# Modulation products in four column strips of TensorE, the first norm in two halves, and row broadcasts by transposes

## Chip, cores and metric

One core of one Trainium2 chip. The metric is the device time of one execution in microseconds, the median of several runs.

## The reference, cut to what matters

Two transformer blocks run one after the other on 256 tokens of width 1024, each of two layers, all in float32. The first has two streams, x (256 tokens) and ctx (256 tokens), and modulates its norms with vectors that come from two condition vectors c and c_ctx:

```
silu_c = silu(c);  silu_cc = silu(c_ctx)
for l in range(2):
    mod   = silu_c  @ w_mod[l] + b_mod[l]          # 6 * 1024 values
    mod_c = silu_cc @ w_mod[l] + b_mod[l]
    sh1, sc1, g1, sh2, sc2, g2 = split(mod, 6)      # the same of mod_c
    h  = rms_norm(x,   norm1[l]) * (1 + sc1)  + sh1
    hc = rms_norm(ctx, norm1[l]) * (1 + csc1) + csh1
    ... = split(h @ w_in[l]), split(hc @ w_in[l])   # q, k, v of two attentions, gates
    x  = x + g1 * branch_merge(attention a, attention b, gates)
    x  = x + g2 * swiglu(rms_norm(x, norm2[l]) * (1 + sc2) + sh2)   # ctx alike in layer 0
return second_block(rms_norm(x, final_norm))
```

The second block has per layer a feed-forward part, a mixer of three attentions, and another feed-forward part, with RMS norms and no modulation.

## The kernel before

Activations lie transposed: 128 partitions by 8 k-tiles by tokens. A float32 product of full accuracy is made of three products of the faster type fp32r: every operand is split into a high part (`hi`, ScalarE, line 403) and a remainder (`lo`, VectorE, line 408), and `group` (with `matmuls`, line 427) issues high x high, high x low and low x high. Weights come from HBM in pieces of up to 1024 columns of float32 per partition (`Weights.raw`, line 341, issued on SyncE's queue, tag "raw", five buffers), and `Weights.next` splits them into eight buffers of high and eight of low parts.

The modulation vectors are products of two rows (the silu of c and of c_ctx, `self.sc`) with w_mod, 512 columns at a time, made in three ways. `mod_columns` makes ten column groups of layer 0. Eight of them go through the split: the stationary operand is `self.scr` (four columns: two high, two low), the moving one is the high and then the low part of the weights, 16 matmuls of 512 columns in all. Two (numbers 1 and 3 of the first four, `MOD_EXACT`, line 610) use plain float32, with `self.sc` (two columns) as the stationary operand. Either way the result is copied to SBUF (line 620), brought into columns by four transposes (line 623), added up by a reduction (line 625) and given its bias (`mod_bias`, line 644). The other columns (layer 0's last two groups and all of layer 1) are multiplied on VectorE (`mod_rest`), and the change doesn't touch them.

`mod_first` makes the first four groups (shift of k-tiles 0 to 3, scale of 0 to 3, shift of 4 to 7, scale of 4 to 7), loads stream x ahead of the first and ctx ahead of the second (`load_x`: load, sums of squares by transposes, reciprocal root by Newton steps, multiply), and works out the amplitude after each pair. `block1` then calls `norm_mod` for each stream, which goes through four blocks of two k-tiles and writes the high and low part of the norm. `b1_attention` then runs layer 0's tokens in the order of `B1_ORDER[0]`: it begins with the value product V1 (k-tiles in order, first stream x, then ctx), and among the later tokens M0 to M5 are the other six groups of `mod_columns` (weights "wm1").

`rows` turns two columns of 128 numbers into rows that are the same on all partitions: a float32 matmul with the column, broadcast along the free dimension, as the stationary operand and the identity as the moving one (line 542). It is called for every reciprocal root that is spread (`spread`), in `keys` and in `forget_rows` of the mixer. `b1_keys` has the same form four times (line 928).

Instructions are put in order by a scheduler that simulates the engines, on the basis of program order and readiness; each engine then runs its own list strictly in that order.

Of the kernel before, what the change touches and what calls it, by code (L numbers as in the profile page):

```python
# [30 lines left out]

BANKS = {"mm": 3, "s": 2, "y": 3}
NPT = (1, 2)
MOD_EXACT, MOD_X = (1, 3), (0, 1)
SUB = 512


# [155 lines left out]

def pieces(n, kparts):

    most = RAW // n // (SUB // n) * (SUB // n)
    return [min(most, nk - k) for nk in kparts for k in range(0, nk, most)]


# [167 lines left out]
class Builder:  # L367
# [171 lines left out]
    def rows(self, ps, r):  # L539

        for t in range(2):
            i = self.nc.tensor.matmul(  # L542
                ps[:, t * P : (t + 1) * P], r[:, t : t + 1].broadcast_to((P, P)), self.ident, start=True, stop=True
            )
        return i

    def spread(self, r, hold=None):
# [9 lines left out]
        self.hold(1, self.last_step, hold[2])  # L557
        return self.spread(self.r, hold[1])

    def norm_mod(self, l, which, i, x, h, pool, rsb=None):  # L560


        nc, (hh, hl) = self.nc, h
        A, B = self.amp[l][:, i, 8 * which :], self.mod[l][:, i, 24 * which :]
        c = slice(i * SEQ, (i + 1) * SEQ)
        for k in range(0, NKT, 2):
            t = pool.tile([P, 2, SEQ], F32, tag="nt", name=self.u("nt"), bufs=3)
            src = x[:, k : k + 2]
            if rsb is not None:
                nc.vector.tensor_tensor(t, src, rsb.unsqueeze(1).broadcast_to((P, 2, SEQ)), ALU.mult)  # L570
                src = t
            for j in range(2):
                a, b = A[:, k + j : k + j + 1], B[:, k + j : k + j + 1]
                if i or j:
                    nc.scalar.activation(t[:, j], src[:, j], AF.Identity, bias=b, scale=a)  # L575
                else:
                    nc.vector.tensor_scalar(t[:, j], src[:, j], a, b, ALU.mult, ALU.add)
            self.hi(hh[:, k : k + 2, c], t)
            self.last_norm = self.lo(hl[:, k : k + 2, c], t, hh[:, k : k + 2, c])
# [6 lines left out]
    def setup_mod(self):  # L586
        nc, cp = self.nc, self.cp
        self.sc = cp.tile([P, NKT, 2], F32, name="sc")
        a = PAR["c"][0]
        nc.scalar.activation(  # L590
            self.sc, self.par[:, a : a + 16].rearrange("p (w k) -> p k w", w=2), AF.Silu
        )
        self.scr = cp.tile([P, NKT, 4], F32R, name="scr")
        self.hi(self.scr[:, :, 0:2], self.sc)
        self.lo(self.scr[:, :, 2:4], self.sc, self.scr[:, :, 0:2])

        self.mod = [cp.tile([P, 2, 48], F32, name=f"mod{l}") for l in range(2)]

        self.amp = [cp.tile([P, 2, 16], F32, name=f"amp{l}") for l in range(2)]

    def mod_columns(self, w, c, tile, exact=None):

        nc = self.nc
        (ps,) = self.product()
        if exact:
            n = 2
            for kp in range(4):
                t = w.raw(2, 512, "mraw", exact)
                for k in range(2):
                    nc.tensor.matmul(  # L610
                        ps[:n], self.sc[:, 2 * kp + k], t[:, k * 512 : (k + 1) * 512],
                        start=(kp, k) == (0, 0), stop=(kp, k) == (3, 1), skip_group_check=True,
                    )
            w.i += 1
        else:
            n = 4
            wk = w.next()
            self.matmuls([(0, 0, ps[:n], self.scr[:, k], a) for k in range(NKT) for a in wk(k)])
        row = tile("mrow")[:n]
        nc.scalar.copy(row, ps[:n])  # L620
        tp = self.bank("y")
        for i in range(4):
            nc.tensor.transpose(tp[:, n * i : n * i + n], row[:, i * P : (i + 1) * P], self.ident[:n, :n])
        a, b = c // P, c // P + 4
        nc.vector.tensor_reduce(
            self.mod[0][:, :, a:b], tp[:, : 4 * n].rearrange("p (j h c) -> p c j h", h=n // 2, c=2), AX.X, ALU.add
        )
        self.mod_bias(0, a, b, 2)

    def mod_first(self, pool):  # L630

        w = Weights(self, "wm0")
        tile = lambda name: pool.tile([P, 512], F32, tag=name, name=self.u(name), bufs=2)
        for i, c in enumerate(MOD_FIRST):
            if i in MOD_X:
                self.load_x(MOD_X.index(i), pool)
            self.mod_columns(w, c, tile, pool if i in MOD_EXACT else None)
            if i % 2:
                self.amplitude(0, 0, 2, slice(2 * i - 2, 2 * i + 2))

    def mod_bias(self, l, c0, c1, nw):
        b = self.p(f"bmod{l}")[:, c0:c1]
# [153 lines left out]
    def block1(self, layers, fill):  # L796
        nc = self.nc
        with self.open("y0") as yp:
            y = self.y_tiles(yp, 2 * SEQ)
            w = Weights(self, "wb1_0")  # L800
            with self.open("h0") as hp:
                h = self.inputs_of(hp)
                with self.open("n0", "right") as np_:
                    self.xs = []
                    self.mod_first(np_)
                    for i, x in enumerate(self.xs):
                        self.norm_mod(0, 0, i, x, h, np_)
                with self.open("a0", "right") as self.ap_:
                    gates = self.b1_attention(0, w, *h, y, 2 * SEQ, yp)
            self.xs, self.xstack = [], ExitStack()  # L810
# [103 lines left out]
    def b1_keys(self, l, w, full, cos, sin):  # L914
# [10 lines left out]
        pr = self.bank("y")  # L925
        for t in range(4):
            o = slice(t * P, (t + 1) * P)
            nc.tensor.matmul(pr[:, o], rw[:, o], self.ident, start=True, stop=True)
        nc.vector.tensor_tensor(kc, kc, pr, ALU.mult)
        self.rope(kc[:, :SEQ], kc[:, :SEQ], cos, sin, SWAP1)  # L930
        return self.stack_k(kc, 512)
# [878 lines left out]
```

## Time and profile before

| | us |
|---|---|
| median of 3 runs | 2501.16 (2499.57 to 2503.38) |
| the profiled execution | 2499.92, span 2498.1 |
| TensorE busy | 2440.1 (98%) |
| VectorE busy | 1836.9 (74%) |
| ScalarE busy | 1373.1 (55%) |
| HBM read | 389.42 MB, 156 GB/s over the span |

In a row of a window the engines stand in the order PE, PEld, DVE, ACT, POOL (GpSimd). PE is TensorE, PEld its weight loads, DVE is VectorE, ACT ScalarE, SPq SyncE's queue of DMA issues. The span is that of the instructions of one execution; the execution's own time lies 1.8 us above it. The granted clock of TensorE (PEclk) is given as a share of full speed: 1.00 is 2.4 GHz, and a lower mean over a stretch says for how much of it the engine had the lower of its two levels, 1.2 GHz. A matmul's record lasts longer than its share of the array's time, since the next starts before it ends; the distance between two starts is what it costs amid other work.

### The profile page before, as it was taken

Reading aid. Unit: us, or ns where it says so; the run is one execution under the profiler, and the core shown is the slowest. Engines: PE = TensorE matmul, PEld = TensorE weight load, DVE = VectorE, ACT = ScalarE, POOL = GpSimd, SP = SyncE. Lnnn points to the kernel's source line nnn. Section 1 sums busy time; section 2 is a strip of 40 time slices with the busy share of each in tenths; the row PEclk is TensorE's granted clock in tenths of the full one; section 3 lists DMA queues with packets and bytes.
Section 4 is the critical chain, followed back from the end, with each engine's and each line's share of the span. In section 5 each row is a group of like instructions: output and inputs, shape, how many; then the busy total and the mean of one; then the engine's idle time right before and its main releaser. Section 6 shows DMA issues by size and latency. Waiting matters only on the chain.

```text
span 2498.1 us, 46101 instructions
## 1 busy us (share of the span) xinstructions
PE 2440.1 (98%) x17342; PEld 2257.4 (90%) x17342; DVE 1836.9 (74%) x4131; ACT 1373.1 (55%) x2683; POOL 0.2 (0%) x4
## 2 busy tenths in 40 slices
PE   8999999999999999999999999999999999999997
PEld 4877768888888898999999999999999999999997
DVE  6677886885766889876676687786666668778665
ACT  5566763422233667665555566755555556665553
POOL 0000000000000000000000000000000000000000
PEclk9999999999999999999999999999999999999999
DMA  7221453454654433565555553356666655336553
GB/s 265 92 72 56 147 178 137 159 184 141 208 183 135 127 115 106 155 187 182 182 185 182 184 182 109 113 178 186 181 186 186 183 180 184 100 116 190 184 180 102
DMA packets 112543, 393.46 MB, mean 157 GB/s; under 512 B 12480, under 2 KB 13760, under 8 KB 111808
## 3 DMA queue, kind: packets, MB, share of 16 engines
q1 hardware_dynamic: 112320, 390.52, 49.1%
q8 instruction: 136, 2.23, 0.4%
q14 instruction: 87, 0.71, 0.1%
HBM read 389.42 MB, written 1.05 MB: 156 GB/s over the span
## 4 chain that ended last, share of the span: by engine, by line
PE 95%; DVE 3%; ACT 2%; issue 0%; DMA 0%; SPq 0%; DVEq 0%; ACTq 0%
PE mm L427 84%; PE y L427 2%; PE s L427 2%; PE s L778 1%; PE y L785 1%; PE s L731 1%; PE y L542 1%; PE y L486 0%; PE mm L610 0%; PE y L678 0%; ACT nt L575 0%; DVE lwmx L408 0%; ACT k L403 0%; DVE kl L408 0%; DVE lwm L408 0%
## 5 line engine op out<-in xcount | busy, mean ns | idle before, releaser
L427 PE MATMUL mm<-hh,hwb 128*128 128x512 f32 (+2 forms) x1176 | 348.5, 341 | 2.6 <-ACT gt L1008 1.4
L427 PE MATMUL mm<-hl,hwb 128*128 128x512 f32 (+1 forms) x1176 | 347.5, 340 | 0.1
L427 PE MATMUL mm<-hh,lwb 128*128 128x512 f32 (+2 forms) x1176 | 347.0, 340 | 0.0
L403 ACT ACTIVATE hwb<-wb_0r 128x512 fp32r<-128x512 f32 (+1 forms) x250 | 149.6, 611 | 253.0 <-PE mm L427 243.5
L427 PE MATMUL mm<-gh,hwf 128*128 128x256 f32 x1344 | 269.5, 281 | 0.0
L427 PE MATMUL mm<-gh,lwf 128*128 128x256 f32 x1344 | 269.1, 281 | 0.0
L427 PE MATMUL mm<-gl,hwf 128*128 128x256 f32 x1344 | 268.4, 281 | 0.0
L408 DVE TENSOR_TENSOR lwf<-wf_1r,hwf 128x512 fp32r<-128x512 f32 (+1 forms) x272 | 183.4, 676 | 109.1 <-ACT hwf L403 100.1
L408 DVE TENSOR_TENSOR lwf<-wf_0r,hwf 128x512 fp32r<-128x512 f32 (+1 forms) x272 | 183.3, 675 | 102.9 <-ACT hwf L403 93.1
L403 ACT ACTIVATE hwf<-wf_1r 128x512 fp32r<-128x512 f32 (+1 forms) x272 | 168.2, 619 | 162.9 <-PE mm L427 149.3
L403 ACT ACTIVATE hwf<-wf_0r 128x512 fp32r<-128x512 f32 (+1 forms) x272 | 168.2, 619 | 162.2 <-PE mm L427 146.5
L427 PEld LDWEIGHTS mm<-hh,hwb 128*128 128x128 f32 x1176 | 204.0, 189 | 29.0 <-ACT gt L1008 2.4
L408 DVE TENSOR_TENSOR lwb<-wb_0r,hwb 128x512 fp32r<-128x512 f32 (+1 forms) x250 | 163.4, 665 | 86.2 <-ACT hwb L403 83.3
L427 PEld LDWEIGHTS mm<-hl,hwb 128*128 128x128 f32 x1176 | 203.7, 189 | 25.5 <-DVE hl L408 0.7
L427 PEld LDWEIGHTS mm<-hh,lwb 128*128 128x128 f32 x1176 | 204.1, 189 | 25.0
L403 ACT ACTIVATE hwb<-wb_1r 128x512 fp32r<-128x512 f32 (+1 forms) x242 | 146.2, 611 | 112.2 <-PE mm L427 101.6
L427 PEld LDWEIGHTS mm<-gh,hwf 128*128 128x128 f32 x1344 | 206.4, 188 | 0.0
L427 PEld LDWEIGHTS mm<-gh,lwf 128*128 128x128 f32 x1344 | 206.4, 188 | 0.0
L427 PEld LDWEIGHTS mm<-gl,hwf 128*128 128x128 f32 x1344 | 206.1, 188 | 0.0
L408 DVE TENSOR_TENSOR lwb<-wb_1r,hwb 128x512 fp32r<-128x512 f32 (+1 forms) x242 | 158.3, 666 | 63.2 <-ACT hwb L403 60.1
L427 PE MATMUL mm<-gl,hwmx 128*128 128x256 f32 x656 | 138.9, 289 | 3.3 <-DVE gl L408 3.3
L427 PE MATMUL mm<-actl,hwf 128*128 128x256 f32 x704 | 141.8, 283 | 0.0
(414 smaller groups left out, 5680.9 us busy)
## 6 DMA issues: line engine op xcount, KB each, us to landing
wf_0r<-in_wf_dram SPq DMA_DIRECT2D x120, 512.0 KB, 3.6
wf_1r<-in_wf_dram SPq DMA_DIRECT2D x120, 512.0 KB, 3.5
wb_0r<-in_wb_dram SPq DMA_DIRECT2D x108, 512.0 KB, 3.7
wb_1r<-in_wb_dram SPq DMA_DIRECT2D x105, 512.0 KB, 3.6
wmx_0r<-in_wmx_dram SPq DMA_DIRECT2D x49, 512.0 KB, 3.6
wmx_1r<-in_wmx_dram SPq DMA_DIRECT2D x49, 512.0 KB, 3.6
wm2r<-in_wm_dram SPq DMA_DIRECT2D x48, 512.0 KB, 3.5
wm1r<-in_wm_dram SPq DMA_DIRECT2D x24, 512.0 KB, 4.0
```

The source lines that it names most:

```text
L403: self.nc.scalar.activation(out, src, AF.Copy, scale=scale)
L408: return self.nc.vector.tensor_tensor(out, src, h, ALU.subtract)
L427: i = nc.tensor.matmul(out, lhsT, rhs, start=bank not in first, stop=n[bank] == 0, skip_group_check=True)
L542: i = self.nc.tensor.matmul(ps[:, t * P : (t + 1) * P], r[:, t : t + 1].broadcast_to((P, P)), self.ident, start=True, stop=True)
L731: nc.tensor.matmul(out, q[a], k[b], start=start and n == 0, stop=stop and n == 2, skip_group_check=True)
L778: nc.tensor.matmul(s[:, :nk], q[:, o], part, start=n == 0, stop=n == 1, skip_group_check=True)
L785: nc.tensor.transpose(tp[:, j * P : (j + 1) * P], pt[:, j * P : (j + 1) * P], self.ident)
```

## The change

All ten groups of `mod_columns` become plain float32 products. The stationary operand is `self.scp`, the two silu columns padded with zeros to 32, and k-tile k writes its products into partitions 32 (k mod 4) to 32 (k mod 4) + 31 of the PSUM bank, which is the strip of 32 columns of the array at the same place; k-tiles 4 to 7 add to those of 0 to 3. The copy takes all 128 partitions, and four float32 products with `self.four` (ones at the places of the four strips) add the strips and bring them into columns. Two additions with the bias read the result from PSUM. The weights go from the load buffers straight to TensorE: the first four groups have eight buffers of their own (tag "mraw"), the six of attention use the five of tag "raw". `mod_first` loads both streams ahead of the first group and calls `norm_mod` for k-tiles 0 to 3 of both streams after the second group, for 4 to 7 after the fourth. In `rows` and `b1_keys` the matmul with the identity becomes TensorE's transpose of the same operand.

```diff
-MOD_EXACT, MOD_X = (1, 3), (0, 1)
@@ def rows
-            i = self.nc.tensor.matmul(
-                ps[:, t * P : (t + 1) * P], r[:, t : t + 1].broadcast_to((P, P)), self.ident, start=True, stop=True
-            )
+            i = self.nc.tensor.transpose(ps[:, t * P : (t + 1) * P], r[:, t : t + 1].broadcast_to((P, P)), self.ident)
@@ def norm_mod
-        for k in range(0, NKT, 2):
+        for k in ks:
@@ def setup_mod
-        self.scr = cp.tile([P, NKT, 4], F32R, name="scr")
-        self.hi(self.scr[:, :, 0:2], self.sc)
-        self.lo(self.scr[:, :, 2:4], self.sc, self.scr[:, :, 0:2])
+        self.scp = cp.tile([P, NKT, 32], F32, name="scp")
+        nc.vector.memset(self.scp, 0.0)
+        nc.vector.tensor_copy(self.scp[:, :, :2], self.sc)
+        self.four = cp.tile([P, 2], F32, name="four")
+        nc.vector.tensor_tensor(self.four, self.ident[:, 0:2], self.ident[:, 32:34], ALU.add)
+        for j in (64, 96):
+            nc.vector.tensor_tensor(self.four, self.four, self.ident[:, j : j + 2], ALU.add)
@@ def mod_columns
-        if exact:
...
-        else:
-            n = 4
-            wk = w.next()
-            self.matmuls([(0, 0, ps[:n], self.scr[:, k], a) for k in range(NKT) for a in wk(k)])
-        row = tile("mrow")[:n]
-        nc.scalar.copy(row, ps[:n])
+        for k in range(NKT):
+            if k % 2 == 0:
+                t = w.raw(2, 512, *pool)
+            j, o = k % 4, 512 * (k % 2)
+            nc.tensor.matmul(
+                ps[32 * j : 32 * j + 32], self.scp[:, k], t[:, o : o + 512], start=k < 4, stop=k >= 4,
+                skip_group_check=True,
+            )
+        w.i += 1
+        row = tile("mrow")
+        nc.scalar.copy(row, ps)
         tp = self.bank("y")
-        for i in range(4):
-            nc.tensor.transpose(tp[:, n * i : n * i + n], row[:, i * P : (i + 1) * P], self.ident[:n, :n])
-        a, b = c // P, c // P + 4
-        nc.vector.tensor_reduce(
-            self.mod[0][:, :, a:b], tp[:, : 4 * n].rearrange("p (j h c) -> p c j h", h=n // 2, c=2), AX.X, ALU.add
-        )
-        self.mod_bias(0, a, b, 2)
+        self.matmuls([(0, i, tp[:, 2 * i : 2 * i + 2], row[:, i * P : (i + 1) * P], self.four) for i in range(4)])
+        a = c // P
+        for i in range(2):
+            nc.vector.tensor_tensor(
+                self.mod[0][:, i, a : a + 4], tp[:, i:8:2], self.p("bmod0")[:, a : a + 4], ALU.add
+            )
@@ def mod_first
-            if i in MOD_X:
-                self.load_x(MOD_X.index(i), pool)
-            self.mod_columns(w, c, tile, pool if i in MOD_EXACT else None)
+            if i == 0:
+                for x in range(2):
+                    self.load_x(x, pool)
+            self.mod_columns(w, c, tile, "mraw", pool, RAW, 8)
             if i % 2:
                 self.amplitude(0, 0, 2, slice(2 * i - 2, 2 * i + 2))
+                for x in range(2):
+                    self.norm_mod(0, 0, x, self.xs[x], h, pool, ks=(2 * i - 2, 2 * i))
@@ def block1
-                    self.mod_first(np_)
-                    for i, x in enumerate(self.xs):
-                        self.norm_mod(0, 0, i, x, h, np_)
+                    self.mod_first(np_, h)
@@ def b1_keys
-            nc.tensor.matmul(pr[:, o], rw[:, o], self.ident, start=True, stop=True)
+            nc.tensor.transpose(pr[:, o], rw[:, o], self.ident)
```

`pieces` also takes at least one k-tile per load now.

## Rows read from the trace of the kernel before

**Rows 1.** The page's busy shares: engine, busy us, share of the span, instructions

```profile
PE 2440.1 (98%) x17342; PEld 2257.4 (90%) x17342; DVE 1836.9 (74%) x4131; ACT 1373.1 (55%) x2683; POOL 0.2 (0%) x4
```

**Rows 2.** The page's chain that ended last, shares by engine

```profile
PE 95%; DVE 3%; ACT 2%; issue 0%; DMA 0%; SPq 0%; DVEq 0%; ACTq 0%
```

**Rows 3.** Windows of the opening: bounds, length, busy us (instructions), PEclk, DMA share, GB/s

```profile
0.00:10.00 10.00, 1.66 (x6) 0.72 (x7) 2.42 (x9) 4.60 (x9) 0.20 (x4) 1.00 0.78 287
10.00:20.00 10.00, 9.49 (x31) 3.04 (x32) 9.53 (x35) 6.48 (x12) 0.00 (x0) 1.00 1.03 422
20.00:30.00 10.00, 10.00 (x33) 2.64 (x32) 7.76 (x25) 4.87 (x11) 0.00 (x0) 1.00 1.02 416
```

**Rows 4.** DMA issues: count, KB each, median us to landing

```profile
wm0r<-in_wm_dram SPq DMA_DIRECT2D x16, 512.0 KB, 10.0
```

**Rows 5.** Timeline of the opening: start, us, engine, line, output and inputs, [idle before]

```profile
40.23 0.56 ACT L620 COPY mrow<-mm 2x512 f32<-2x512 f32 x1
...
42.67 0.41 PE L623 MATMUL y<-const,mrow 2*128 2x2 f32 x4
...
43.71 2.07 ACT L575 ACTIVATE nt<-xin,mod,amp 128x256 f32<-128x256 f32 x4 [2.93 <-DVE amp L649]
...
50.86 1.90 DVE L408 TENSOR_TENSOR hl<-nt,hh 128x512 fp32r<-128x512 f32 x3 [2.63 <-ACT hh L403]
...
57.42 0.31 PE L427 MATMUL mm<-hwb,hl 128*128 128x320 f32 x1
```

**Rows 6.** Plain f32 products: all (ns min/median/max), then weight loads in time

```profile
L610 PE MATMUL mm<-wm0r,sc x32: 591/592/592, 17.2 to 39.0; 128*2 128x512 f32 x32
...
33.22 0.08 PEld L610 LDWEIGHTS mm<-wm0r,sc 128*2 128x2 f32 x1 [0.34 <-issue]
...
33.65 0.09 PEld L610 LDWEIGHTS mm<-wm0r,sc 128*2 128x2 f32 x1 [0.34 <-issue]
```

**Rows 7.** Timeline of TensorE where a split modulation group begins in attention

```profile
261.56 0.39 PE L427 MATMUL mm<-hh,lwb 128*128 128x512 f32 x1
261.79 0.40 PE L427 MATMUL mm<-hwm,scr 128*4 128x512 f32 x1
262.02 0.40 PE L427 MATMUL mm<-lwm,scr 128*4 128x512 f32 x1
```

**Rows 8.** Attention's modulation weights: ns min/median/max, first and last start; landing in us

```profile
L403 ACT ACTIVATE hwm<-wm1r x48: 612/629/635, 242.1 to 346.7; 128x512 fp32r<-128x512 f32 x48
...
L408 DVE TENSOR_TENSOR lwm<-wm1r,hwm x48: 672/685/694, 242.9 to 347.6; 128x512 fp32r<-128x512 f32 x48
...
L341 SPq DMA_DIRECT2D wm1r<-in_wm_dram x24: 327/328/328, 175.8 to 330.3; - x24
...
DMA to landing us min/median/max: 3.3/4.0/5.3
```

**Rows 9.** Windows of layer 0's attention

```profile
180.00:200.00 20.00, 16.57 (x71) 12.24 (x71) 14.71 (x44) 11.43 (x29) 0.00 (x0) 0.83 0.00 1
310.00:320.00 10.00, 6.32 (x23) 2.63 (x22) 9.93 (x24) 8.32 (x19) 0.00 (x0) 0.83 0.61 211
```

**Rows 10.** Pieces of the chain: start, us, engine, output, line, records

```profile
451.09 0.44 PE y L542 x4
...
484.07 0.44 PE y L678 x4
...
2486.68 0.42 PE y L486 x2
...
2489.53 1.21 PE y L542 x4
```

**Rows 11.** Broadcast products by form: count, busy us, mean ns, idle before

```profile
L542 PE MATMUL y<-const,rcol 128*128 128x128 f32 x76 | 13.6, 298 | 5.3 <-DVE rcol L536 5.3
...
L542 PE MATMUL y<-const,ccol 128*128 128x128 f32 x48 | 6.7, 277 | 0.0
```

More of the change, by code (lines that the diff above doesn't have):

```diff
@@ L194, in pieces @@
 def pieces(n, kparts):
-    most = RAW // n // (SUB // n) * (SUB // n)
+    most = max(RAW // n // (SUB // n) * (SUB // n), 1)
     return [min(most, nk - k) for nk in kparts for k in range(0, nk, most)]
@@ L558, in rstd_rows, with norm_mod @@
         return self.spread(self.r, hold[1])
-    def norm_mod(self, l, which, i, x, h, pool, rsb=None):
+    def norm_mod(self, l, which, i, x, h, pool, rsb=None, ks=range(0, NKT, 2)):
         nc, (hh, hl) = self.nc, h
@@ L597, in setup_mod, with mod_columns @@
         self.mod = [cp.tile([P, 2, 48], F32, name=f"mod{l}") for l in range(2)]
         self.amp = [cp.tile([P, 2, 16], F32, name=f"amp{l}") for l in range(2)]
-    def mod_columns(self, w, c, tile, exact=None):
+    def mod_columns(self, w, c, tile, *pool):
         nc = self.nc
         (ps,) = self.product()
-        if exact:
[L606 to L612, printed above, removed]
-                    )
-            w.i += 1
-        else:
-            n = 4
-            wk = w.next()
-            self.matmuls([(0, 0, ps[:n], self.scr[:, k], a) for k in range(NKT) for a in wk(k)])
-        row = tile("mrow")[:n]
-        nc.scalar.copy(row, ps[:n])
-        tp = self.bank("y")
-        for i in range(4):
-            nc.tensor.transpose(tp[:, n * i : n * i + n], row[:, i * P : (i + 1) * P], self.ident[:n, :n])
-        a, b = c // P, c // P + 4
-        nc.vector.tensor_reduce(
-            self.mod[0][:, :, a:b], tp[:, : 4 * n].rearrange("p (j h c) -> p c j h", h=n // 2, c=2), AX.X, ALU.add
-        )
-        self.mod_bias(0, a, b, 2)
@@ L630, in mod_first @@
-    def mod_first(self, pool):
+        for k in range(NKT):
[9 more added lines that the diff above has]
+        nc.scalar.copy(row, ps)
+        tp = self.bank("y")
+        self.matmuls([(0, i, tp[:, 2 * i : 2 * i + 2], row[:, i * P : (i + 1) * P], self.four) for i in range(4)])
@@ L632, in mod_first @@
+        a = c // P
[3 more added lines that the diff above has]
+            )
+    def mod_first(self, pool, h):
         w = Weights(self, "wm0")
```

## Prediction

> **What bounds the kernel now.** I read the busy shares first, then the chain that ended last, then the stages that the change touches. TensorE is busy in 2440.1 us of a span of 2498.1 [rows 1] and carries 95% of the chain [rows 2]; VectorE and ScalarE are at 74% and 55%. So a saving on VectorE or ScalarE is worth something only where TensorE waits for them, and a saving on TensorE is worth nearly its own size. There are two places where TensorE is not the limit. In the opening the DMA engines are full: their share of the windows from 10 to 30 us is 1.03 and 1.02 [rows 3]. In layer 0's attention TensorE sits idle in patches, as in 180 to 200 us (16.57 busy of 20, granted clock 0.83) and 310 to 320 us (6.32 of 10, clock 0.83, VectorE 9.93 of 10) [rows 9].
>
> **Part 1, the opening.** What ends it is the value product V1: its last matmul starts at 57.42 [rows 5]. Before it stand the four column groups of the modulations, two in split form and two in plain f32, then the norm. The loads needed are 16 of 512 KB [rows 4] and the two streams of 1 MB each (128 x 8 x 256 x 4 bytes, by the code): 10.5 MB. The first three windows moved 2.87 + 4.22 + 4.16 = 11.25 MB [rows 3], so with these loads first in the queue the last lands at about 28.5 us, and a column group (four loads, 2.1 MB at some 0.42 MB per us) arrives every 5.0 us.
>
> The price of a column group on TensorE is the disputed number. An f32 product is two matmul records: 32 records stand for 16 products [rows 6]. Weight loads follow each other at 33.22 and 33.65, so one pass over 512 columns takes 0.43 us and its narrow weight load 0.08 [rows 6]. Eight k-tiles in a row would be 16 x 0.43 = 6.9 us; four abreast without loss 4 x 0.43 = 1.7, some 2.0 with the tail of 0.16 that 0.59 against 0.43 shows [rows 6] and the weight loads. No row of before shows two products side by side, so these are the bounds. I take a value between, for this reason: in the timelines TensorE's records follow one another, none starting ahead of its predecessor [rows 6, 7], and the two passes of a k-tile stand next to each other. The second pass needs the columns that the first still uses; the next k-tile, in other columns, stands behind it. So only the second pass of one k-tile can run beside the first pass of the next: 9 steps of 0.43 = 3.9 us, or 8 x (0.43 + 0.08) + 0.43 = 4.5 with the weight loads in the open. I take 4.2, under the 5.0 of the loads, so TensorE keeps up.
>
> The Trainium skill, TensorE: Matmul & The Clock Gate, Part 3 (The mechanism; Measured speedup), has matmuls start and end strictly in order, which is the step just made, and three column tiles together 2.38 times as fast. By that factor a group would cost about 2.9 us, an estimate from its figure, and the six groups of attention 8 us less than I take.
>
> The last group then ends at about 30.5. Copy 0.56, small products, two additions and the amplitude: before, the norm's first ScalarE work starts 3.5 us after the copy starts (40.23 to 43.71), of which about 1.4 is the small products standing behind V1's matmuls until 42.67 [rows 5]. So the second half of the norm starts at about 32.6. Before, six blocks of the norm were left at that point and took 43.71 to 52.76; now four are left: 6.0 us, to 38.6. V1 ended 5.0 us after the last block (52.76 to 57.73) [rows 5]: 43.6 now, 14 us sooner. Against it: V1's own weights now land behind the modulations, and their conversions share ScalarE and VectorE with the norm. Loading both streams first costs the modulations one more 1 MB transfer, 2.5 us, which the byte count already has. I take **-9**, with -4 and -14 as ends.
>
> **Part 2, the six groups in attention.** Now each is 16 matmuls at 0.23 (261.79 to 262.02) [rows 7] and four transposes at 0.11 [rows 10]: 4.1 us. After, 4.2 and eight records at about 0.11 (the f32 products with "four"; nearest row, the broadcast products, 0.44 for four [rows 10]): 5.1. TensorE pays +1.0 each, **+6**. ScalarE loses 48 conversions of 0.629 (30 us) and VectorE 48 of 0.685 (33 us) [rows 8]. Worth something in 310 to 320 us alone: idle 3.7 and clock 10 x 0.17 = 1.7, together 5.4, of which I take **-5**. The loads of these groups are issued from 175.8, but the first conversion is at 242.1 [rows 8]; without conversions their products can fill holes like 180 to 200 us, where 3.4 us are idle and 20 x 0.17 = 3.4 go with the clock [rows 9]: **-4**. Together -3, with -16 (full overlap) and +15 (none) as ends. "pieces" changes nothing for the widths in use.
>
> The Trainium skill, TensorEngine Tiling (Array Packing), Key Properties, speaks against this part: a change of tiling mode drains TensorE. The row shows no gap between a full-width product and one with four columns (261.56 to 261.79, the same 0.23) [rows 7], though whether that pair changes the mode can't be seen. Were the 0.16 tail exposed twice in each of six groups, the sum would be 2 us worse.
>
> **Part 3, rows by transposes.** A broadcast product in f32 is four records for two blocks, 0.44 us amid other work; four transposes take the same 0.44 [rows 10], and a pair at the very end is "x2" where the broadcast is "x4": a transpose is one record. So a call falls from 0.44 to 0.22. There are 76 / 4 + 48 / 4 = 31 calls [rows 11], 6.8 us; b1_keys' two calls fall from eight records to four, 0.9 more. The last one stands alone on the chain, 1.21 against 0.42 for a pair of transposes [rows 10], worth 0.8 by itself. Some stand where TensorE waits anyway, so I take **-6.5**, with -3 and -8 as ends.
>
> Dropping the split of the silu vector, the memset and the four additions for "four" lie beside the first load and cost nothing; without that cover they would be under 1 us. Two additions replace a reduction and two additions.
>
> **Sum:** -9 - 3 - 6.5 = -18.5 against the profiled run's 2499.92 gives 2481.4; the median of the runs, 2501.16, lies 1.2 above that run, so the forecast is **2482.5**.
>
> **Rivals.** *Full overlap* (0.22): the four column strips take both passes without waiting. 2.2 us less for each of six groups and 1 less in the opening: about 2468.5. For it: the change keeps neighbours in different columns. Against: the in-order starts.
> *No overlap* (0.25), the one on the other side: products in different columns run one after the other, 6.9 us a group. Attention then pays 6 x (6.9 + 0.9 - 4.1) = +22, less about 7 for relief and holes; the opening becomes TensorE's, 4 x 6.9 = 28 us from the first load on beside 5 us of norms, and gains nothing; the transposes stay. +15 - 6.5 = +8.5: about 2510. It decides from about 5 us a group (the loads' pace); near 6 the sum is nil. For it: the trace has no two products side by side.
> *Buffers* (0.08): a load buffer was free after its conversion; now the products of attention hold it until TensorE, in order, has read it, and the weights of the next tokens queue behind on SyncE. At a landing of 4.0 us [rows 8], half of it exposed in each of six groups is +12: about 2494.5. Against it: the DMA share there is far from full in most windows.
>
> **How the numbers follow.** Forecast 0.45. A measurement of this kernel can tell about 0.2%, 5 us. Faster (under 2496.2): 0.43 of the forecast, all of full overlap, 0.05 of buffers, 0.02 of no overlap: 0.72. Same: 0.02 + 0.03 + 0.08 = 0.13. Slower (over 2506.2): 0.15 of no overlap. The range runs from 2466, a little below full overlap, to 2510, the middle of no overlap, since half of that case is all that may be left out; the forecast's own range is 2472 to 2493, by the ends of its parts.
>
> **What would show it.** The starts of a group's 16 records: every 0.43 (no overlap), in pairs (two abreast, 3.9 to 4.5 us a group), or in bunches of four (full). V1's end near 48 instead of 57.4. Between 10 and 28 us a DMA share near 1 with TensorE waiting for loads. Broadcasts as "x2" of 0.22. In attention no f32r conversions for these groups, and no stretch like 310 to 320. I am wrong if V1's end hasn't moved (loads late, or the norm's ScalarE work is the bound), if new idle patches behind loads appear after 240 us, or if the order that the scheduler finds elsewhere moves by more than the parts.

## The result and the profile after

| | median of the runs, us | lowest to highest | span of the profiled run |
|---|---|---|---|
| before | 2502.08 | 2499.57 to 2503.38 | 2498.1 |
| after | 2472.98 | 2472.36 to 2473.78 | 2472.0 |

The ratio is 0.9885, with a 95% interval of 0.9868 to 0.9902: 29 us less. The forecast was 2482.5, in a range of 2466 to 2510. So the time lies in the range, on the right side, and 9.5 us under the forecast; the terms of the sum did worse than the sum, as the last sections show.

Two lines of the page of after, the busy shares and the chain by engine, answer to [rows 1, 2]. TensorE is busy 26.6 us less and is still nearly the whole chain.

```profile
PE 2413.5 (98%) x17312; PEld 2240.0 (91%) x17312; DVE 1798.8 (73%) x4061; ACT 1340.7 (54%) x2618; POOL 0.2 (0%) x4
...
PE 93%; DVE 4%; ACT 2%; issue 1%; DMA 0%; SPq 0%; DVEq 0%; ACTq 0%
```

**A column group in attention.** TensorE's timeline of after (start, us, engine, line, operation, records) where a group stands between other products:

```profile
278.03 0.28 PE L426 MATMUL y<-pth,vs 128*128 128x256 f32 x1
278.15 0.38 PE L785 MATMUL y<-const,pt 128*128 128x128 f32 x2
278.64 1.92 PE L612 MATMUL mm<-wm1r,scp 128*32 128x512 f32 x16
280.50 0.39 PE L426 MATMUL y<-ptl,vs 128*128 128x256 f32 x1
```

From its first start to the start of what follows it takes 1.85 us; I had 4.2. Its single records come in bunches of four, 6 to 7 ns apart within a bunch: at 278.641, .648, .655, .661, then four from 279.095, four from 279.524 and four from 279.953, so one bunch every 0.43 us. That is the full overlap of my first rival. Two more of the six groups look the same; three are cut into two pieces by other products between them, of 1.84 and 0.98 us (once 0.98 and 1.85). The six take 14.0 us together, 2.3 each.

**The opening.** Three windows of after that answer to [rows 3] (bounds, length, busy us of PE, PEld, DVE, ACT, POOL, then granted clock, DMA share, GB/s), then SyncE's issues, then the work behind the last load:

```profile
0.00:10.00 10.00, 1.21 (x4) 0.58 (x4) 3.08 (x13) 3.76 (x6) 0.20 (x4) 1.00 0.75 290
10.00:20.00 10.00, 9.78 (x44) 3.11 (x46) 7.61 (x34) 3.20 (x7) 0.00 (x0) 1.00 1.03 413
20.00:30.00 10.00, 7.63 (x32) 4.20 (x30) 8.47 (x33) 3.85 (x10) 0.00 (x0) 0.66 1.03 408
```

```profile
2.58 7.29 SPq L340 DMA_DIRECT2D wm0r<-in_wm_dram  x8
10.82 5.46 SPq L340 DMA_DIRECT2D wb_0r<-in_wb_dram  x5
17.29 8.73 SPq L340 DMA_DIRECT2D wm0r<-in_wm_dram  x8
...
37.30 1.06 PE L612 MATMUL mm<-wm0r,scp 128*32 128x512 f32 x8
38.78 1.05 PE L612 MATMUL mm<-wm0r,scp 128*32 128x512 f32 x4
41.34 0.95 PE L426 MATMUL y<-four,mrow 128*128 128x2 f32 x8
...
42.72 2.08 ACT L572 ACTIVATE nt<-xin,mod,amp 128x256 f32<-128x256 f32 x4 [2.25 <-DVE amp L649]
...
54.21 0.31 PE L426 MATMUL mm<-hwb,hl 128*128 128x320 f32 x1
```

Five loads of V1's weights stand ahead of the last eight modulation loads, so the last of these lands at 35.9 us (31.3 before; I had 28.5), and the last group runs up to 39.8, not 30.5. The last half of the norm starts at 42.72 (before 43.71), with four blocks to do where before there were six, and V1's last product starts at 54.21 (57.42 before [rows 5]): 3.2 us sooner where I had 9.

**The rows.** A group of the view by form, then a piece of the chain near its end: 38 records for the 76 of [rows 11], each as long as one of those, and 0.68 us with two records for 1.21 with four [rows 10].

```profile
L541 PE MATMUL y<-const,rcol 128*128 128x128 f32 x38 | 9.0, 296 | 7.4 <-DVE rcol L535 7.4
```

```profile
2463.91 0.68 PE y L541 x2
```

**Something I had not looked for.** In the feed-forward parts TensorE is 100% busy before and after, at full clock, on the same products. Windows of 80 us in the first such part of the second block, before, then after:

```profile
1291.00:1371.00 80.00, 80.00 (x679) 80.00 (x678) 54.71 (x95) 45.33 (x79) 0.00 (x0) 1.00 0.57 188
```

```profile
1276.00:1356.00 80.00, 80.00 (x708) 80.00 (x707) 56.76 (x98) 46.84 (x81) 0.00 (x0) 1.00 0.60 195
```

708 products for 679 in the same time. Nothing of the change is in this stretch, and it is worth 4 us there (the lead over before grows from 14.6 us ahead of this part to 19.1 behind it).

### The profile page after: what moved, and what is told of

Read it like the earlier page. It is cut to its first block, busy times and chain, and to the rows that moved or that the text cites. A ratio compares the mean times of both kernels' runs of the same rounds, so it can differ in the third digit from the quotient of the medians.

```text
span 2472.0 us, 45820 instructions
## 1 busy us (share of the span) xinstructions
PE 2413.5 (98%) x17312; PEld 2240.0 (91%) x17312; DVE 1798.8 (73%) x4061; ACT 1340.7 (54%) x2618; POOL 0.2 (0%) x4
## 4 chain that ended last, share of the span: by engine, by line
PE 93%; DVE 4%; ACT 2%; issue 1%; DMA 0%; SPq 0%; DVEq 0%; ACTq 0%
PE mm L426 83%; PE y L426 2%; PE s L426 2%; PE s L778 1%; PE s L731 1%; PE y L785 1%; PE mm L612 1%; PE y L485 0%; DVE lwb L407 0%; PE y L678 0%; ACT pt L755 0%; DVE kl L407 0%; ACT pth L402 0%; DVE ptl L407 0%; ACT nt L572 0%
## 5 line engine op out<-in xcount | busy, mean ns | idle before, releaser
L426 PE MATMUL mm<-gh,hwmx 128*128 128x256 f32 x656 | 140.9, 290 | 3.0 <-DVE kl L407 3.0
```

The costliest lines, as they stand in the source:

```text
L426: i = nc.tensor.matmul(out, lhsT, rhs, start=bank not in first, stop=n[bank] == 0, skip_group_check=True)
```

## The experiments

Differences are taken against the kernel before as timed on the same chip: 2501.13 beside rows_only, attn_only, one_strip and pad, 2502.47 beside mix, same_strip, after_32 and after_128, 2502.04 beside mix_first_128, attn_rows, before_1056 and old_order.

### Do the strips run side by side, and what makes them?

**one_strip**: the whole change with all k-tiles in the first strip.

```diff
-            j, o = k % 4, 512 * (k % 2)
+            o = 512 * (k % 2)
-                ps[32 * j : 32 * j + 32], self.scp[:, k], t[:, o : o + 512], start=k < 4, stop=k >= 4,
+                ps[:32], self.scp[:, k], t[:, o : o + 512], start=k == 0, stop=k == NKT - 1,
```

> The changed kernel with all eight k-tiles of a modulation group in the same 32 columns, one after the other; all else as in the changed kernel. Theory that the strips run side by side: the 16 passes of a group now start every 0.43 us, 6.9 us a group in place of 1.9; six groups in attention add up to 30 us of which holes hide some, and the opening becomes TensorE's: 2490 to 2505 against 2473 of the changed kernel. Rival, that the gain in attention comes from the conversions that went and not from the strips: no more than 2480.

Measured: 2515.84 us (2513.16 to 2516.88), ratio 1.0055 (1.004 to 1.007). A group is now a row of starts 0.43 us apart:

```profile
297.53 7.05 PE L612 MATMUL mm<-wm1r,scp 128*32 128x512 f32 x16
304.51 0.50 PE L426 MATMUL mm<-hh,hwb 128*128 128x512 f32 x1
```

6.98 us for 1.85. Side by side is worth 2515.84 - 2472.98 = 43 us: the six groups of attention take 42.7 us together instead of 14.0, which is 29, and V1 ends 10 us later than in after. That is more than the 2490 to 2505 that I expected, since no holes hid any of the 29. Without the strips the change would have made the kernel slower by 14.7 us. My rival on the other side had the price of a group right (6.9); its time of 2510 was too low, for its opening was to gain nothing and V1 ends 7 us later than before (64.56 for 57.42).

**same_strip**: the whole change with neighbouring k-tiles in one strip (0,0,1,1,2,2,3,3).

```diff
-            j, o = k % 4, 512 * (k % 2)
+            j, o = k // 2, 512 * (k % 2)
-                ... start=k < 4, stop=k >= 4,
+                ... start=k % 2 == 0, stop=k % 2 == 1,
```

> The whole change, with neighbouring k-tiles in the same strip of columns (0,0,1,1,2,2,3,3 instead of 0,1,2,3,0,1,2,3); the sums are the same. Theory 'in order' (products start in program order and run side by side only because their neighbours use other columns; the two passes of a product and the two k-tiles of a strip follow each other): 13 steps of 0.43 us, 5.6 us a group instead of 1.85, so some 20 us for the six groups in attention and up to 10 in the opening: 2495 to 2505. Rival 'a line for each strip' (a strip works off its own products whatever stands ahead in the other strips): four steps, 1.85 us a group, the time of the whole change within 3 us.

Measured: 2484.57 us (2481.57 to 2490.57), ratio 0.9925 (0.9908 to 0.9942): 11.6 us over after, between the two theories. The trace settles it. A group that is issued in one go:

```profile
289.02 1.94 PE L612 MATMUL mm<-wm1r,scp 128*32 128x512 f32 x16
290.90 0.39 PE L426 MATMUL y<-pth,vs 128*128 128x256 f32 x1
```

It takes 1.87 us, as with neighbours apart, and its 16 records come in four bunches of four (13 ns apart within a bunch where after has 6 to 7, since only every second product opens a strip; so the products do stand in the order 0,0,1,1,2,2,3,3). The second, third and fourth record of the first bunch each wait for the semaphore of a load of their own: they are k-tiles 2, 4 and 6. Each strip has four passes to do one after the other; for all to end after four steps, strips 1 to 3 must have begun while the second k-tile of strip 0, ahead of them in the program, still waited for its columns. So **a strip works off its own products and does not wait for those ahead in other strips**: the rival. My two abreast rested on the opposite. The Trainium skill, TensorE: Matmul & The Clock Gate, Part 3 (The mechanism), has matmuls start and end strictly in program order; for plain f32 products in four strips of columns these starts differ from it, and the measurement decides. The 11.6 us have another cause. Four of the six groups are cut into pieces, and a piece of two k-tiles (one load) takes 0.98 us where these stand in two strips but 1.83 where they stand in one. The six take 20.6 us together, 6.6 more than in after, and V1 ends 3.6 us later. (This trace is of the slowest of the four executions, 16.8 us over that of after, so these figures don't split up the 11.6 exactly: in it layer 0's attention takes 11.3 us more than in after, and 2 us are lost behind it.)

### What are the parts worth?

**rows_only**: before, with the transposes in `rows` and `b1_keys` alone.

```diff
-            i = self.nc.tensor.matmul(
-                ps[:, t * P : (t + 1) * P], r[:, t : t + 1].broadcast_to((P, P)), self.ident, start=True, stop=True
-            )
+            i = self.nc.tensor.transpose(ps[:, t * P : (t + 1) * P], r[:, t : t + 1].broadcast_to((P, P)), self.ident)
...
-            nc.tensor.matmul(pr[:, o], rw[:, o], self.ident, start=True, stop=True)
+            nc.tensor.transpose(pr[:, o], rw[:, o], self.ident)
```

> The kernel before with the broadcasts of rows and b1_keys as transposes, nothing else. Theory: the change's third part is worth about 6 us, spread over the heads of the feed-forward parts and the mixers: some 2496 against 2502, and TensorE's pace in the first feed-forward part of the second block stays at 678 records in 80 us as in the kernel before. Rival: the transposes are worth nothing amid other work (within 2 us of before). Second rival: the faster pace there (708 records in 80 us in the changed kernel) comes with the transposes, then about 2491.

Measured: 2492.16 us (2490.62 to 2492.48), ratio 0.9961 (0.9946 to 0.9976), 9.0 us. TensorE's busy time fell from 2440.1 to 2432.4, by 7.7: 6.8 + 0.9, the whole of what I had counted before I took something off for calls that stand where TensorE waits. The pace in the feed-forward part stays at 678 in 80 us, so the transposes alone don't bring the 708.

**attn_only**: before, with the new column groups for the six groups of attention alone.

```diff
+    def mod_strips(self, w, c, tile, *pool):    # mod_columns of the change
...
-            self.mod_columns(wm, 2048 + 512 * n, self.t2)
+            self.mod_strips(wm, 2048 + 512 * n, self.t2)
```

> The kernel before with the four strips in the six modulation groups of attention alone; the opening and the broadcasts as before. Theory: attention ends 10 us earlier, about 2492 against 2502. Rival, that the groups gained because the opening's shift changed the order in attention: no more than 3 us.

Measured: 2474.51 us (2473.59 to 2475.79), ratio 0.9893 (0.9877 to 0.991): 26.6 us, nearly the whole change, and far more than either theory. In its trace layer 0's first feed-forward silu starts at 441.57, only 9.6 us sooner than before; most of the rest comes in the second block, where 708 products stand in 80 us in the first feed-forward part and in the third too. So attention itself gave some 10 us at most, as the theory had it, and the rest asked for a test of its own.

### Where do 708 products for 679 come from?

The single records show what happens. In after, the products of the first feed-forward part start 117 to 119 ns apart up to 1268.6; then two transposes of `rows` come between; from 1269.1 on they start 113, 113, 114 ns apart, in the same order of operands, and keep to that for 768 products, up to 1356.0, where the products that stream another operand (acth) begin. Timeline of TensorE in after at that place:

```profile
1268.53 0.40 PE L426 MATMUL mm<-gh,lwf 128*128 128x256 f32 x2
1268.76 0.38 PE L541 MATMUL y<-const,rcol 128*128 128x128 f32 x2
1268.90 0.48 PE L426 MATMUL mm<-gh,hwf 128*128 128x256 f32 x2
1269.21 0.39 PE L426 MATMUL mm<-gl,hwf 128*128 128x256 f32 x2
```

Before, no more than five products in a row are 115 ns or less apart. What differs there is where the weight buffers (of the split weights, and the tiles behind them) lie in SBUF: the change's new tiles moved their start from 39680 to 40608 bytes. The streamed operands gh and gl lie at the other end of SBUF and stay where they were.

**pad**: before, with 928 unused bytes ahead of the weight buffers (they start at 40608 as in after).

```diff
+        pad = cp.tile([P, 232], F32, name="pad")
+        nc.vector.memset(pad, 0.0)
```

> The kernel before with 928 bytes per partition of unused constants, which move the tiles behind them as far as the changed kernel's new constants do. Theory that the pace of the first feed-forward part of the second block hangs on where tiles lie: 708 records in 80 us as in the changed kernel in place of 678, and about 2497. Rival, that it hangs on the order or the number of instructions: 678 records, and within 1 us of the kernel before.

Measured: 2498.0 us (2495.78 to 2502.31), ratio 0.9987 (0.9978 to 0.9997), and 682 products in the window where before has 679. The effect is there, but it isn't the 708.

**after_32** and **after_128**: the whole change with the same edit and 8 and 32 columns, so that the weight buffers start at 40640 and at 40736.

> The whole change with 32 unused bytes ahead of the weight buffers, so that these start at 40640 in SBUF, a multiple of 64 as before the change (39680), instead of 40608. Theory 'placement' (the shorter spacing of the 256-column products, 117.8 or 113.3 ns for 118.3, comes from where the change put the weight buffers): the mean spacing goes back to 118.3, no feed-forward call has 708 records in 80 us, and the time is some 7 us over that of the whole change, near 2480. Rival 'rhythm' (it is the products' own rhythm, taken up at a restart and independent of the placement): 708 records in some call as before, and the time within 2 us of the whole change.

> The whole change with 128 unused bytes ahead of the weight buffers, which then start at 40736 as in the kernel with the new groups in attention alone, where the spacing of 113.3 ns was met three times as often. Theory 'placement': 113.3 ns in the first and the third feed-forward call and in patches of the mixers, about 3000 products at 4.4 ns less, and a time 8 to 10 us under the whole change, near 2464. Rival 'rhythm': which stretch has it is unrelated to the placement, and the time is within 3 us of the whole change.

Measured: after_32 2473.69 us (2472.21 to 2475.22), ratio 0.9886 (0.9871 to 0.99), and after_128 2463.07 us (2461.84 to 2463.96), ratio 0.9843 (0.9828 to 0.9857). Windows in the first feed-forward part of after_32, and in the first and the third of after_128:

```profile
1276.00:1356.00 80.00, 80.00 (x688) 80.00 (x687) 55.40 (x95) 45.92 (x80) 0.00 (x0) 1.00 0.57 189
```

```profile
1276.00:1356.00 80.00, 80.00 (x707) 80.00 (x707) 56.32 (x97) 47.02 (x83) 0.00 (x0) 1.00 0.59 193
1864.00:1944.00 80.00, 80.00 (x709) 80.00 (x708) 56.31 (x96) 47.03 (x82) 0.00 (x0) 1.00 0.63 193
```

128 unused bytes make the kernel 10 us faster, as "placement" had it. With 32 bytes the stretches of 113 are gone, also as it had it, but its 118.3 did not come back: 116.7 ns in the first and third part instead, and the time of after. So each placement has its own set of spacings, and my rule of multiples of 64 is wrong. Nor does the start alone decide: at 40608, after, mix, old_order, one_strip and same_strip have 113.3 in the first part, and pad has 117.8 in all four. What in the change makes that difference (the two transposes at the restart are one candidate) wasn't tested.

**before_1056**: before, with the same edit and 264 columns: 1056 unused bytes, nothing else.

> The kernel before, with 1056 unused bytes ahead of the weight buffers and nothing else, so that these start at 40736 as in after_128. Theory 'placement alone': some 3000 products of 256 columns at 113.3 ns for 118.3 and the rest at 117.8 or so, 15 us less than before, near 2487. Rival 'placement and load' (the shorter spacing needs the new groups as well, which leave ScalarE, VectorE and the weight buffers alone): not more than 500 such products and 2496 to 2500, as with 928 bytes.

Measured: 2484.58 us (2483.28 to 2487.07), ratio 0.9932 (0.9916 to 0.9949): 17.5 us from 1056 bytes that nobody reads, as "placement alone" had it:

```profile
1291.00:1371.00 80.00, 80.00 (x709) 80.00 (x707) 57.69 (x99) 46.83 (x82) 0.00 (x0) 1.00 0.58 189
1895.00:1975.00 80.00, 80.00 (x708) 80.00 (x707) 56.33 (x97) 47.30 (x81) 0.00 (x0) 1.00 0.62 191
```

With that, the spacing can be taken out of every comparison. The mean distance between starts of neighbouring 256-column products (some 12,000 distances of 109 to 127 ns in each trace) times 12,500, a little over the number of neighbouring pairs in a trace (12,260 to 12,285), against that of before:

| kernel | weight buffers start at | mean distance, ns | spacing, us | measured, us | measured less spacing, us |
|---|---|---|---|---|---|
| before | 39680 | 118.37 | | | |
| rows_only | 39680 | 118.40 | +0.3 | -9.0 | -9.3 |
| pad | 40608 | 118.08 | -3.6 | -3.1 | +0.5 |
| before_1056 | 40736 | 116.86 | -18.9 | -17.5 | +1.4 |
| attn_only | 40736 | 116.87 | -18.8 | -26.6 | -7.8 |
| attn_rows | 40736 | 116.78 | -19.9 | -36.7 | -16.8 |
| after | 40608 | 117.78 | -7.4 | -29.1 | -21.7 |
| after_32 | 40640 | 117.70 | -8.4 | -28.8 | -20.4 |
| after_128 | 40736 | 116.81 | -19.5 | -39.4 | -19.9 |
| one_strip | 40608 | 117.76 | -7.6 | +14.7 | +22.3 |

pad and before_1056, which change nothing else, come out within 1.4 us of zero, so I take the last column as good to some 1.5 us, though the intervals of the single ratios are wider (about 3.7 us to either side). And the parts add up: rows 9.3 and attention 7.8 make 17.1, and attn_rows, which has both, 16.8. Two pairs with the same start need no spacing taken out: attn_only is 9.1 us under before_1056, and after_128, the whole change, 21.9 (by the column "measured").

### What did the opening gain, and why not 9?

**old_order**: the whole change, but the streams' loads stand where they stood before and the norm comes after the fourth group.

```diff
-            if i == 0:
-                for x in range(2):
-                    self.load_x(x, pool)
+            if i < 2:
+                self.load_x(i, pool)
...
-                for x in range(2):
-                    self.norm_mod(0, 0, x, self.xs[x], h, pool, ks=(2 * i - 2, 2 * i))
```

> The whole change without the new order in the opening: the streams' loads stand ahead of the first and the second group and the norm comes after the fourth, as before; the column groups there are the new ones. It tells what the new groups and what the new order bring in the opening. Theory 'order' (before, six blocks of the norm were left when the last amplitude was there, and now four; this is nearly all of the 3.2 us): V1's end near 57, as before, and 3 us over the whole change, near 2476. Rival 'groups' (the conversions that fell away are what made V1 earlier): V1's end within 1 us of 54.2 and the same time.

Measured: 2480.21 us (2479.62 to 2484.43), ratio 0.9915 (0.99 to 0.993): 7.2 us over after, and its V1 ends 2.7 us later than before:

```profile
60.07 0.31 PE L426 MATMUL mm<-hwb,hl 128*128 128x320 f32 x1
```

V1's end is not the same in every trace of one opening. The six kernels with the opening of before have 57.4 to 59.2, and after, after_32 and after_128 have 52.9 to 54.2, so the change's opening is worth about 5 us at V1 rather than 3.2. The new order is then worth 6 to 7 us at V1, and the new groups without it cost 1 to 3 (their last load lands at 36.5, before's at 31.3): the theory "order" had the sign, and more than it asked for.

**attn_rows**: before's opening, with the new groups in attention and the transposes.

> The opening of before, with the new column groups in attention and the rows by transposes; its weight buffers start at 40736, as in the run after_128, so the two differ in the opening alone. Theory 'parts' (after the products' spacing is taken out, attention is worth 7 us, the rows 9, and what is left of the change, the opening, 5): 2468, 5 us over after_128. The prediction's own step had 9 for the opening: 2472. Rival 'opening for nothing' (its gain is made up for later): within 2 us of after_128.

Measured: 2465.30 us (2463.17 to 2466.39), ratio 0.9851 (0.9836 to 0.9865). after_128 has the same placement and is 2.2 us faster, so the change's opening is worth 2 us net, on the edge of what can be told, and nearer to the rival's "within 2" than to the 5 of "parts". By the last column of the table it is 3 to 5. Its V1 ends 5.8 us later than that of after_128, and the two are still 5.3 us apart at the end of layer 0; they are 2.6 apart behind layer 1's attention, and level behind the second mixer. Where the lead goes is seen (the traced execution of attn_rows is the fastest of its four); why those two stages turn out 2 to 3 us shorter in one kernel than in another is not settled. In two other pairs a lead at V1 lasts to the end: after over old_order (5.9 at V1, 6.1 at the end of the traces) and mix_first_128, below, over after_128 (4.0 and 3.9).

**mix**: the whole change, with the third group's loads in the ring of the other weights.

```diff
-            self.mod_columns(w, c, tile, "mraw", pool, RAW, 8)
+            self.mod_columns(w, c, tile, *(() if i == 2 else ("mraw", pool, RAW, 8)))
```

> The whole change, with one edit: the third of the four column groups in the opening takes its loads in the weights' own ring instead of the eight-buffer ring, so that twelve of the sixteen modulation loads stand ahead of V1's weights in SyncE's queue instead of eight. Theory 'queue' (the opening gained 3.2 us instead of 9 because eight modulation loads were issued at 17.29 and later, behind five loads of V1's weights): the last modulation load lands some 5 us earlier, V1's last product starts near 49 instead of 54.2, and the time is 3 to 5 us under that of the whole change. Rival 'clock and norm' (the granted clock of 0.66 and the norm's ScalarE blocks set the end whatever the loads do): V1 moves by less than 1 us and the time is the same within 1 us.

Measured: 2471.08 us (2468.98 to 2473.87), ratio 0.9876 (0.9861 to 0.9891). The last modulation load was issued at 21.0 instead of 25.7, it landed at 31.5 instead of 35.9, and V1's end moved by 0.5 us, less than it differs between traces of one opening: the theory "queue" alone falls. SyncE's issues, then TensorE's and ScalarE's rows in mix:

```profile
2.58 12.26 SPq L340 DMA_DIRECT2D wm0r<-in_wm_dram  x12
...
17.12 4.16 SPq L340 DMA_DIRECT2D wm0r<-in_wm_dram  x4
...
38.84 1.06 PE L612 MATMUL mm<-wm0r,scp 128*32 128x512 f32 x8
...
42.20 2.08 ACT L572 ACTIVATE nt<-xin,mod,amp 128x256 f32<-128x256 f32 x4 [0.92 <-DVE amp L649]
```

The last half of the last group still ran at 38.84, behind V1's first products in TensorE's order, which ran from 35.00 to 38.84 at a granted clock of 0.53, so almost wholly at the lower level.

**mix_first_128**: mix, with V1's products ordered behind the last modulation product, and the 128 bytes of after_128.

```diff
+        self.last_mod = last        # in mod_columns, the last strip product
...
+        self.held[0].append([0, 96, self.last_mod])        # at the end of mod_first
```

> The whole change with three edits: 128 unused bytes ahead of the weight buffers (as in the run after_128, 2463.07), the third group's loads in the weights' ring (as in the run mix), and V1's products ordered behind the last modulation product on TensorE. In the run mix the last modulation load had been issued at 21.0 us, yet the last eight records of the fourth group stood behind V1's first products and ran at 38.84. Theory 'order': with TensorE's order mended as well, the second half of the norm starts near 36 instead of 42.2 and V1's last product near 48 to 49; the time is some 5 us under that of after_128, near 2458. Rival 'clock and ScalarE': the granted clock falls to half in another place and ScalarE, which had the two halves of the norm and V1's conversions to do, becomes late; V1's end at 52 or later and the time within 2 us of after_128.

Measured: 2458.31 us (2456.83 to 2459.64), ratio 0.9824 (0.9809 to 0.9838), 4.8 us under after_128; the forecast of "order" was 2458. The same rows as for mix, and V1's last product:

```profile
32.21 1.07 PE L615 MATMUL mm<-wm0r,scp 128*32 128x512 f32 x8
...
35.96 0.95 PE L426 MATMUL y<-four,mrow 128*128 128x2 f32 x8
...
37.34 2.08 ACT L572 ACTIVATE nt<-xin,mod,amp 128x256 f32<-128x256 f32 x4 [1.59 <-DVE amp L654]
...
48.85 0.31 PE L426 MATMUL mm<-hwb,hl 128*128 128x320 f32 x1
```

V1's end at 48.85 is 8.6 us sooner than before, once both queues have the order that the sum took for granted. In time, this kernel is 7.0 us under attn_rows, which has the opening of before, the same start of the buffers and the same rest: that, and not 9, is what the opening was seen to give. It beats both before and after, by 44 and 15 us; 10 of the 15 come from the 128 bytes.

## Why the prediction was right, and where its steps failed

**The total** was right in part by luck: three terms were off, two of them too small and one too large, and a fourth was missing. Against my -9, -3 and -6.5 the runs show some -2 to -5, -8 and -9. These misses nearly cancel out: the three make -19 to -22, where I had -18.5. The spacing adds -7.4, which no step of mine had, and makes up most of the 9.5 us by which the forecast missed. The four together, from -26 to -29, are what was measured.

**Price of a group (4.2 us).** The failing step is the sentence that the next k-tile, in other columns, "stands behind it", the second pass. I had read from [rows 6, 7] that no record starts ahead of its predecessor; but those products all use the same columns, so the rows could not have shown anything else. one_strip and same_strip show the rule for strips: 6.98 us in one strip, 1.85 in four, whatever the order. My pass of 0.43 us was right, and the bound of 2.0 that I called "four abreast without loss" was the answer. Of the tail that I had feared twice a group some 0.1 us shows behind it: in after, what follows starts 0.52 us after the last record's start (279.973 to 280.495), and a pass takes 0.43.

**Attention (-3).** With 2.3 a group as it came, TensorE's own share is 6 x (2.3 + 0.9 - 4.1) = -5.4. Relief and holes, for which I had taken 9 us, brought about 2.6: TensorE's idle time in the stretch of the groups is 120 - 115.85 = 4.15 us before (260 to 380) and 110 - 108.40 = 1.6 in attn_only (260 to 370). Together -8.0, and -7.8 was measured by the table, -9.1 against before_1056. (Not in this sum: before had the lower clock from 314.4 to 317.8, which can cost 1.7 us at most, and attn_only did not.) The holes failed outright: the first product on these weights runs at 257.3, and the counterpart of 180 to 200 us [rows 9] is as idle as before. The relief came in its place (9.61 busy for 6.32, full clock for 0.83). Windows of before and of attn_only for the idle time, then two of after, to be read against [rows 9]:

```profile
260.00:380.00 120.00, 115.85 (x587) 85.29 (x586) 99.08 (x247) 80.44 (x176) 0.00 (x0) 0.99 0.55 185
...
260.00:370.00 110.00, 108.40 (x608) 81.76 (x606) 72.89 (x196) 56.26 (x130) 0.00 (x0) 1.00 0.53 195
```

```profile
175.00:195.00 20.00, 16.56 (x74) 12.39 (x73) 15.45 (x47) 12.49 (x30) 0.00 (x0) 0.83 0.01 1
300.00:310.00 10.00, 9.61 (x67) 5.42 (x60) 8.44 (x22) 7.06 (x16) 0.00 (x0) 1.00 0.87 315
```

**Opening (-9).** The failing step is "with these loads first in the queue". The change gives the loads a ring of eight buffers, the sixteen loads need it twice, and SyncE goes on with V1's weights meanwhile; that could have been read from the diff. A second assumption failed behind it, that TensorE would take the last group as soon as it landed. The first repair alone gives 0.5 us at V1 (mix); both together give 8.6 at V1 and 7.0 in time (mix_first_128); the second alone wasn't run. What the change gained came from its new order (old_order), in which four blocks for six stand behind the last amplitude; the streams' loads ahead of the groups and the norm by halves weren't tested apart.

**Rows (-6.5).** The mechanism and its full count of 7.7 held; the deduction for calls that stand in a wait was not needed, and 9.0 was measured, just past my end of -8; the 1.3 between them is within the interval of that ratio.

**The rivals.** Full overlap (0.22, 2468.5) was the mechanism of the strips. Its time lies 4.5 us under the measured one, and without the spacing it would be 12 under, since my opening and my holes were in it, which gave less. No overlap was ruled out, at a price of a group which one_strip confirms. Buffers: no wait for these loads shows up in attention. And of what I said would prove me wrong, one thing happened: stages elsewhere moved by more than the parts, and mainly not through the order of the work but through its placement.

## What to carry to other kernels

Narrow products cost a full pass over the moving columns each (0.43 us for 512, with 2 stationary columns [rows 6] or 32); put in different strips of columns they run four at a time even in plain f32, and what counts is how many strips a load's k-tiles fill, not the order of the neighbours. An earlier end of a chain needs the order of every queue on it, and a ring smaller than its loads gives SyncE's place away to what comes next. Before a change of a few tenths of a per cent is put down to its mechanism, compare the spacing of untouched products: here a shift of the buffers by 128 or 1056 bytes was worth 10 and 17 us.

## What the runs showed of the hardware that I had not expected

- Four f32 products in four strips of columns start 6 to 7 ns apart, and a strip that is busy doesn't hold up the others (1.85 and 1.87 us a group for both orders).
- Full-width 256-column products that follow each other without a wait have several spacings at full clock, by the mean of a feed-forward part or a stretch of it: 113.3, 116.7, 117.7 and 118.3 ns. The shortest was taken up behind a gap of 0.2 us at transposes of `rows` (after at 1268.9, after_128 at 1853.3) and kept for up to 939 products. Whether it is found depends on where the buffers lie (39680: never for more than five products; 40736: in some 3000 products, in each of five kernels), though not on that alone (40608: 768 products in one go in after, none over 30 in pad). What in the addresses decides it is open, as is why only the first and third feed-forward part take 113.3, though all four use the same buffers.
- In the opening of after, the granted clock fell to 0.50 (the lower level, 1.2 GHz) in the windows from 23 to 29 us, after a stretch in which TensorE waited (0.13 us busy between 21 and 23); before, it did not [rows 3]. There the eight small products of a group took 1.71 us for 0.95.
